# A hybrid layer's recurrences on TensorE: Gated DeltaNet's two directions in one pass, RWKV-7's head halves alternating

## The chip, the cores and the metric

One core of a Trainium2 chip runs the whole program in one launch. The metric is the device time of an execution in microseconds (us). The engines are PE (TensorE: matrix products and transposes), DVE (VectorE), ACT (ScalarE), POOL (GpSimd) and SP (SyncE, whose queue issues most DMAs). PEld is PE's loading of weights, which a trace shows apart. On-chip memory has 128 partitions; PSUM, the memory that products are written to, has eight banks.

## The reference

One layer: a token mixer of four branches on the same modulated input (256 context and 256 latent tokens, 2048 channels), then a gated ConvFFN. Cut to the two branches that the change touches:

```python
def gdn_scan(q, k, v, lg, beta, S):       # both directions stacked; chunks of 64 tokens
    """S_t = a_t S_{t-1}(I - b_t k_t k_t^T) + b_t k_t v_t^T (S: (G,H,dk,dv)), o_t = S_t^T q_t."""
    ...
    def step(S, inp):
        ut, wt, at, qt, kt, glt = inp
        vnew = ut - jnp.einsum('ghld,ghde->ghle', wt, S)
        o = jnp.einsum('ghld,ghde->ghle', qt, S) + jnp.einsum('ghts,ghse->ghte', at, vnew)
        S = S * jnp.exp(glt)[..., None, None] + jnp.einsum('ghld,ghle->ghde', kt, vnew)
        return S, o

def rwkv_scan(r, w, k, v, a, b, S):       # 8 heads of 64
    def step(S, inp):
        rt, wt, kt, vt, at, bt = inp
        sa = jnp.einsum('ghij,ghj->ghi', S, at)
        S = S * wt[:, :, None, :] + sa[..., None] * bt[:, :, None, :] + vt[..., None] * kt[:, :, None, :]
        return S, jnp.einsum('ghij,ghj->ghi', S, rt)
```

DeltaNet has 4 heads of 128 channels; the forward direction takes the chunks in order, the backward one in reverse, first over the context (no outputs wanted), then over the latent tokens from the state the context left. The other branches are a convolution module and a bidirectional mLSTM. Their four outputs are projected, weighted by sigmoid gates, summed (the merge) and projected once more.

## The kernel before

Everything large is a product with streamed weights. A weight block is loaded as `raw` through SP's queue, ACT rounds it to `hi` (line 192), DVE takes the rest `lo` (line 194), and PE multiplies three times: hi by the input's high part (`uh`), hi by its low part (`ul`), lo by `uh`. Results with weights stationary are psB, with activations stationary psA. adaLN's products (psw) are spread between them. The recurrences are in plain fp32; each fp32 product appears in the trace as two records, a transpose as one.

The order on each engine is set by the framework's scheduler, which lists the instructions by simulated times of its own. The recurrences are given to it with priority, and what is left of PE's time is filled with column sets: psB for the branches' columns, psA for the gates, and, beside the mLSTM, the merges.

- RWKV-7 (`rw_unit`, `rw_step`, both directions' chunks in turn): `rw_unit` prepares one chunk of 64 tokens. The 8 heads lie as 4 pairs (h) on two halves of the partitions (q). For each q, four products psG (one PSUM bank for each q, tag "u", which has two banks), a masked copy G on DVE, a copy to AL on ACT; then four transposes psT for each q. 16 units in all. psS, psY and psSA, in `rw_step`, are written with h outside and q inside.
- DeltaNet (`gd_scan`): two segments (context, latent) of four chunks. In each, for i in 0 to 3 and each direction d: pKS = K S (4 heads), gX = V - decay pKS on DVE, pVN = U gX (U: a triangular inverse made before), gVN = beta pVN, for the latent segment pQS = Q S and pO = att gVN, both into the output `go`, then pSn = K^T gVN and the new state gS on DVE. A chunk's rows lie on the half of the partitions given by the chunk's parity; direction d at step i uses one half alone, and the DVE instructions run on 64 partitions. Kd and V are loaded for two chunks (128 tokens) at a time.
- mLSTM (`ml_scan`): four chunks of 128 in two half steps each (one a direction): psr (row terms), masks mA made by ACT and DVE from psr and the scores psq, psn = mA V, then dn and mlh on DVE. Its output goes through `head_out` (squares mhsq, mhms, transposes psho).
- Merge (`merge`): 16 sets of 24 psA products, in order of the branches RWKV, convolution, DeltaNet, mLSTM. The first branch's sets are written to the accumulator mg (line 1327), the others added on POOL (line 1330) after a product with the gate (line 1329).

Tiles live in pools, stacks of on-chip memory: a pool opened later lies above those still open, and takes over the place of one that has been closed; who takes over a place waits for its last reader.

Of the kernel before, what the change touches and what calls it, by code (L numbers as in the profile page):

```python
# [11 lines left out]
F32 = mybir.dt.float32  # L12
# [3 lines left out]
AF = mybir.ActivationFunctionType  # L16
# [4 lines left out]
P = 128  # L21
# [11 lines left out]
# columns of the per-channel parameters: first one, number  # L33
# [8 lines left out]
class Kern:  # L42
# [4 lines left out]
    # ---------------------------------------------------------------- helpers  # L47
# [13 lines left out]
    def aux(self, name="aux", tag="aux"):  # L61
        """PSUM bank; its tag's banks go round in program order."""
        bufs = self.auxn.get(tag)
        assert bufs, tag
        return self.auxp.tile([P, 512], F32, tag=tag, name=name, bufs=bufs)
# [8 lines left out]
    def evp(self, name):  # L74
        """PSUM behind column sets and adaLN, apart from the recurrences'."""
        return self.wap.tile([P, 512], F32, tag="wa", name=name)
# [3 lines left out]

    def tr(self, out, in_, b=0):
        """out = in_.T; in_ starts at partition b."""
        k = in_.shape[0]
        self.nc.tensor.transpose(out, in_, self.ident[b : b + k, b : b + k])
# [9 lines left out]
    def rsqrt(self, pool, x, shape, tag):  # L94
        """x ** -0.5 in place of a small fp32 tile of positive values (Newton from a bit-level guess)."""
# [6 lines left out]
        # y (15 - 10 a + 3 a^2) / 3 of a = x y^2, then y' (3 - 9/64 x y'^2) 3/16  # L102
# [9 lines left out]
    # ---------------------------------------------------------------- constants  # L112
    def constants(self):
# [15 lines left out]
        # LM[:, kind, col] over (row % 64): 0 col>row, 1 col>=row, 2 col<row, 3 col<=row  # L129
# [7 lines left out]
        # block-diagonal 128x128 versions  # L137
# [19 lines left out]
    def first_params(self):  # L157
        """Per-channel parameters, one column per 128 channels; c and c_ctx first."""
        t = self.cp.tile([P, NVEC], F32, name="vec")
        for sl in (slice(0, 32), slice(32, NVEC)):  # L160
            self.nc.sync.dma_start(out=t[:, sl], in_=self.A["vec"][:, sl])
        self.PC = {nm: t[:, o : o + n] for nm, (o, n) in VEC.items()}

    def params(self):
        nc, PC = self.nc, self.PC
        # a = 1 - mu0 - mu1 of the token shift
# [10 lines left out]
    # ---------------------------------------------------------------- weight stream  # L177
# [3 lines left out]
    def load_split(self, parts, width, rings=None):  # L181
        """parts: [(dram [256, w], column offset)] -> hi, lo tiles [128, 2, 512] in fp32r."""
# [18 lines left out]
    def mode_b_steps(self, parts_of, width, blocks, uh, ul, nkt, bank=None):  # L201
        """Weights stationary: out[channel, token]. blocks: (offset, M, token0, N, evacuate).
        One step per pair of K tiles; the evacuations follow the last."""
# [16 lines left out]
    def mode_a(self, parts_of, uh, ul, nkt, toks, evac, apart=0, rings=None):  # L220
        """Activations stationary: out[token, channel] for 512 channels. apart: this many last steps go by token tile."""
# [19 lines left out]
    # ---------------------------------------------------------------- adaLN  # L241
    def wmod_steps(self, cb, dst, raws=None, gain=None):
        """One step per 256 rows of w_mod[:, 512 cb:][:512]; the last one leaves silu(c) @ it + b_mod in dst, feature-major
        [128, 4, 1 or 2]. The partial sums of column half h lie on rows 64 h + 32 k + {0: c, 1: c_ctx}."""
# [18 lines left out]
        if gain is not None:  # L263
            # a gate vector on every partition, times the norm's gain
# [25 lines left out]
    def mod_feed(self):  # L290
        """Steps of the other four adaLN vectors of the latent stream, taken beside the column sets: shift and scale of the
        FFN feature-major, the gates token-major."""
# [6 lines left out]
    def feed(self, upto=0):  # L299
        """As many adaLN steps as the rate says, and all before step `upto`."""  # L300
# [5 lines left out]
    # ---------------------------------------------------------------- phase 0  # L306
    def phase0(self, first, opened):
        """adaLN shift and scale of the mixer, modulated input u (context tokens first); `first`: the steps of
        column sets that run as its K tiles appear; `opened`: called before their last ones."""
# [38 lines left out]
        # what is left of u takes the place of the token tiles  # L348
# [42 lines left out]
    # ---------------------------------------------------------------- inverse of unit triangular 64x64 blocks  # L391
# [7 lines left out]
    def tinv(self, pool, tag, d, n, N, U, pool_rec=False, ptag="aux"):  # L399
        """U[:, j] = (I - N[:, j])^-1 for n matrices per half of the partitions: rows s on partitions (two blocks  # L400
        of 64), columns t on the free axis; N is read only where t follows s (t > s for d = 0, t < s for d = 1).
        U's off-diagonal block on the other side has to be zero already. A generator: what needs no product first."""
# [78 lines left out]
    # ---------------------------------------------------------------- RWKV-7  # L481
    def shift(self, out3, ps3, nm, i, M):
        """Token shift of out3 [M, segments, 256] from PSUM."""
# [6 lines left out]
    def stage(self, tag, shape, name):  # L490
        """Staging tile behind a column set."""
# [3 lines left out]
    def rw_k_steps(self):  # L495
# [3 lines left out]
        def ev_k(i):  # L499
            def f(ps):  # L500
                k, kk = self.kT[:, i], self.kk[:, i]
                self.shift(s3(k), s3(ps), "", 4 + i, P)
                # -l2_normalize(k * rw_kk) per head
# [14 lines left out]
    def rw_ev_v(self, i):  # L518
        """Evacuation of a block of v: feature-major latent half, token-major to DRAM."""
# [57 lines left out]
    def rw_feat(self):  # L577
        """Decayed operands of all chunks, per direction: dAR [.., chunk, head pair, a | r], dBK [.., b | k | b]."""
# [6 lines left out]
        # 0 at the multiples of 64, 1 elsewhere  # L585
# [5 lines left out]
        for h in range(4):  # L591
# [39 lines left out]
            # bonus = sum over the head of r * (kmod of both directions) * rk, times v  # L631
# [7 lines left out]
    def rw_unit(self, d, ch):  # L639
        """Masked products and triangular inverses of one chunk of 64 tokens."""  # L640
# [13 lines left out]
        G = [wp.tile([P, 4, P], F32, tag="G%d" % i, name="G%d" % i) for i in range(2)]  # L654
        for q in range(2):
            ps = self.aux("psG", "u")
            p3 = ps[:, 0 : 4 * W_].rearrange("p (h t) -> p h t", h=4)
            r, o = half[q], half[1 - q]
            for h in range(4):
                self.mm(p3[:, h], bk[r, h, 64 * q : 64 * q + P], AL[q][r, h, 0:W_])  # L660
            nc.vector.tensor_tensor(G[q][:, :, 0:W_], p3, mb, ALU.mult)
            nc.scalar.activation(AL[q][o, :, 0:W_], G[q][o, :, 0:W_], AF.Copy)
        bkT = wp.tile([P, 2, 4, 64], F32, tag="bkT", name="bkT")
        for q in range(2):
            ps = self.aux("psT", "u")
            p3 = n4(ps)
            for h in range(4):
                self.tr(p3[:, h], bk[half[q], h, 64 * q : 64 * q + P], 64 * q)
            nc.scalar.activation(bkT[:, q], p3, AF.Copy)
# [6 lines left out]
    def rw_sv(self, d, ch):  # L676
        """New [S^T ; V] tile of a chunk: V in place."""
# [6 lines left out]
    def rw_step(self, d, ch, unit, SV, nxt):  # L684
        """One chunk: reads SV, writes the states into the next SV (None behind the last chunk)."""
# [82 lines left out]
    # ---------------------------------------------------------------- branch outputs  # L768
    def put_y(self, n, b, yf):
        """Block b (128 channels) of branch n's output, split for the projection; kept where u's context half was."""  # L770
# [4 lines left out]
    def head_norm(self, pool, tag, h, n_tok, nh, w, eps):  # L775
        """rsqrt(mean(h^2) + eps) over the last axis of h [128, n_tok, nh, w] -> [128, n_tok, nh]."""
# [9 lines left out]
    def head_out(self, pool, tag, h, gate, norm, n):  # L786
        """Branch n = rms_norm(h [128, 2, 4, 128]) * norm * gate [128 channels, 4, 256]."""
# [6 lines left out]
        for b in range(4):  # L794
            ps = self.aux("psho")
            for i in range(2):
                self.tr(ps[:, P * i : P * i + P], h[:, i, b])
# [4 lines left out]
    # ---------------------------------------------------------------- convolution module  # L802
# [41 lines left out]
    def conv_module(self):  # L844
# [26 lines left out]
        for i in range(4):  # L871
            nc.vector.tensor_tensor(acc[:, i], acc[:, i], mean, ALU.subtract)
            sq = cp.tile([P, 256], F32, tag="csg", name="csq", bufs=2)
# [12 lines left out]
    # ---------------------------------------------------------------- gate scalars, token-major  # L886
    def token_gates(self, gp):
        """lg [128, 4 tiles, 8], beta, and mLSTM's li, lf, all (direction, head) on the last axis."""
# [10 lines left out]
        g = gp.tile([P, 4, 2, 2, 2, 4], F32, name="gtok")  # tile, (ml, gd), direction, (i/f or a/b), head  # L899
# [11 lines left out]
        # softplus(x) = max(x, 0) + log1p(exp(-|x|)), log1p(y) = 2 atanh(y / (2 + y))  # L911
# [21 lines left out]
    # ---------------------------------------------------------------- gated DeltaNet  # L933
    def gd_columns(self):
# [56 lines left out]
        def ev_q(h):  # L991
            def f(ps):
# [4 lines left out]
                # sums over the channels, tokens on partitions  # L997
# [10 lines left out]
    def gd_scan(self):  # L1008
# [9 lines left out]
        # decays: inclusive sums, sums after a token, chunk totals  # L1018
# [17 lines left out]
        nc.vector.tensor_scalar(fl(nbeta), fl(beta), -1.0, None, ALU.mult)  # L1036
        self.dbg("egc", egc)
        self.dbg("erem", erem)
        self.dbg("egl", egl)
        N = up.tile([P, 2, 2, 4, 64], F32, name="gN")     # direction, tile of the segment, head, t  # L1040
# [9 lines left out]
        for seg in range(2):  # L1050
# [33 lines left out]
            order = [[0, 1, 2, 3], [3, 2, 1, 0]]  # L1084
            KV = [None, None]
            for i in range(4):
                for d in range(2):
                    c = order[d][i]
                    jj, j = c // 2, 2 * seg + c // 2
                    r = slice(64 * (c % 2), 64 * (c % 2) + 64)  # L1090
                    if i % 2 == 0:
# [577 lines left out]
```

## Time and profile before

| | |
|---|---|
| median of 3 runs | 2360.63 us (2359.28 to 2361.23) |
| profiled execution, span | 2358.9 us |
| PE busy | 2250.4 us (95%) |
| DVE, ACT, POOL busy | 1478.0, 987.1, 500.8 us |
| moved by DMA | 471.97 MB, 200 GB/s on average |
| RWKV's scan (psG, psS and the like) | about 324 to 757 us |
| DeltaNet's steps | 928 to 968 and 1110 to 1230 us |
| mLSTM's scan | about 1290 to 1403 us |

The profiled execution's span lies 1.7 us below the runs' median, 0.4 us below the fastest run. A row of the timeline gives the start, the duration, the engine, the line, the operation and how many records it groups; the time from one row's start to the next one's is what the engine was held for. Line 79 is the helper that issues all products, line 84 the one for transposes.

### The profile page before, as it was taken

To read this page: it belongs to the slowest core of one execution; us is meant where nothing else is said; L and a number is where in the kernel's file an instruction comes from. 1 tells how busy PE (TensorE), PEld (TensorE's weight loads), DVE (VectorE), ACT (ScalarE), POOL (GpSimd) and SP (SyncE) were. 2 spreads that over 40 slices of the span, in tenths; PEclk is the share of its full clock that TensorE was granted. 3 is DMA by queue.
4 is the path that set the end of the run, shared out by engine and by line. 5 is a ranking of instruction groups with operands and counts; after the bars stand their busy time and mean duration, and the time that the engine had idled before them with its cause. 6 is when DMAs were issued, how large, how long until landed. Compare 5 with 4: busy or idle time off the path is not lost.

```text
span 2358.9 us, 42865 instructions
## 1 busy us (share of the span) xinstructions
PE 2250.4 (95%) x16820; PEld 1846.2 (78%) x16820; DVE 1478.0 (63%) x3079; ACT 987.1 (42%) x1491; POOL 500.8 (21%) x849
## 2 busy tenths in 40 slices
PE   6979899999999899999999999989999999999998
PEld 3657677877888666767777777779999999998886
DVE  3357866643555976566556478566777677775554
ACT  4225644433444343233225544444444344444443
POOL 0012563533452995000001034010000000000000
PEclk8989899899999999999999999989999999999999
DMA  9934654454666677677668667567767666666563
GB/s 367 347 113 129 180 166 117 133 169 135 184 180 197 184 239 216 208 238 233 189 206 275 185 223 262 184 224 216 225 210 218 208 182 187 180 199 204 193 195 101
DMA packets 273612, 471.97 MB, mean 200 GB/s; under 512 B 41505, under 2 KB 80673, under 8 KB 272417
## 3 DMA queue, kind: packets, MB, share of 16 engines
q1 hardware_dynamic: 273122, 467.14, 63.6%
q8 instruction: 132, 2.16, 0.4%
q10 hardware_dynamic: 288, 2.10, 0.2%
q14 instruction: 70, 0.57, 0.1%
HBM read 440.33 MB, written 28.84 MB: 199 GB/s over the span
## 4 chain that ended last, share of the span: by engine, by line
PE 80%; DVE 8%; DMA 5%; ACT 2%; POOL 2%; issue 2%; SPq 0%; DVEq 0%; ACTq 0%; POOLq 0%
PE psB L79 35%; PE psA L79 20%; PE psD L79 10%; PE psw L79 4%; DVE lo L194 2%; DMA wraw<-in_w_mod 2%; PE psG L79 1%; DMA raw<-in_w_mix 1%; DVE cacc L858 1%; POOL riU L397 1%; PE pVN L79 1%; PE pKS L79 1%; PE pSn L79 1%; ACT hi L192 1%; PE psf L79 1%
## 5 line engine op out<-in xcount | busy, mean ns | idle before, releaser
L194 DVE TENSOR_TENSOR lo<-raw,hi 128x1024 fp32r<-128x1024 f32 (+2 forms) x485 | 603.6, 1246 | 449.7 <-ACT hi L192 440.2
L192 ACT ACTIVATE hi<-raw 128x1024 fp32r<-128x1024 f32 (+2 forms) x488 | 508.4, 1043 | 845.4 <-PE psB L79 383.7
L79 PE MATMUL psB<-u2h,lo 128*128 128x256 f32 x1408 | 396.7, 283 | 0.0
L79 PE MATMUL psB<-u2l,hi 128*128 128x256 f32 x1408 | 396.5, 283 | 0.2 <-DVE u2l L1354 0.2
L79 PE MATMUL psB<-u2h,hi 128*128 128x256 f32 x1408 | 395.5, 285 | 1.1 <-DVE u2h L1353 1.1
L79 PE MATMUL psA<-lo,uh 128*128 128x512 f32 x832 | 336.3, 405 | 12.6 <-DVE lo L194 12.3
L79 PE MATMUL psA<-hi,ul 128*128 128x512 f32 x832 | 329.8, 397 | 0.0
L79 PE MATMUL psA<-hi,uh 128*128 128x512 f32 x832 | 310.0, 404 | 2.2 <-ACT hi L192 2.2
L79 PE MATMUL psB<-uh,hi 128*128 128x256 f32 (+1 forms) x832 | 281.5, 347 | 24.4 <-ACT hi L192 17.8
L79 PE MATMUL psB<-ul,hi 128*128 128x256 f32 (+2 forms) x832 | 278.9, 340 | 0.0
L79 PEld LDWEIGHTS psB<-u2h,hi 128*128 128x128 f32 x1408 | 267.6, 192 | 10.8 <-issue 9.5
L79 PEld LDWEIGHTS psB<-u2l,hi 128*128 128x128 f32 x1408 | 269.9, 192 | 0.5 <-DVE u2l L1354 0.5
L79 PEld LDWEIGHTS psB<-u2h,lo 128*128 128x128 f32 x1408 | 269.8, 192 | 0.1
L79 PE MATMUL psB<-uh,lo 128*128 128x256 f32 (+2 forms) x832 | 263.1, 342 | 6.8 <-DVE lo L194 6.8
L79 PEld LDWEIGHTS psA<-lo,uh 128*128 128x128 f32 x832 | 156.9, 189 | 63.0 <-DVE lo L194 21.7
L79 PEld LDWEIGHTS psB<-uh,hi 128*128 128x128 f32 x832 | 159.9, 193 | 54.8 <-ACT hi L192 20.7
L79 PEld LDWEIGHTS psA<-hi,uh 128*128 128x128 f32 x832 | 153.5, 189 | 51.5 <-issue 15.0
L79 PEld LDWEIGHTS psA<-hi,ul 128*128 128x128 f32 x832 | 157.0, 189 | 33.6 <-issue 1.0
L79 PEld LDWEIGHTS psB<-uh,lo 128*128 128x128 f32 (+1 forms) x832 | 153.8, 192 | 32.3 <-DVE lo L194 9.6
L79 PEld LDWEIGHTS psB<-ul,hi 128*128 128x128 f32 (+1 forms) x832 | 160.6, 193 | 22.0 <-issue 6.1
L1524 DVE TENSOR_TENSOR lo<-raw,hi 128x1024 fp32r<-128x1024 f32 x88 | 107.6, 1225 | 78.3 <-ACT hi L1523 78.2
L1444 DVE SCALAR_TENSOR_TENSOR facc<-fpad,ffdw,facc 128x256 f32<-128x256 f32 x352 | 152.9, 488 | 0.2
(569 smaller groups left out, 3129.1 us busy)
## 6 DMA issues: line engine op xcount, KB each, us to landing
raw<-in_w_in SPq DMA_DIRECT2D x208, 512.0 KB, 4.5
raw<-in_ffn_up SPq DMA_DIRECT2D x176, 512.0 KB, 3.9
wraw<-in_w_mod SPq DMA_DIRECT2D x160, 512.0 KB, 5.3
raw<-in_ffn_down SPq DMA_DIRECT2D x88, 512.0 KB, 4.6
raw<-in_w_br SPq DMA_DIRECT2D x32, 512.0 KB, 4.8
raw<-in_w_out SPq DMA_DIRECT2D x32, 512.0 KB, 4.7
raw<-in_w_mod SPq DMA_DIRECT2D x32, 512.0 KB, 4.0
raw<-in_w_in SPq DMA_DIRECT2D x48, 256.0 KB, 3.7
```

The costliest lines, as they stand in the source:

```text
L79: self.nc.tensor.matmul(out, lhsT, rhs, start=start, stop=stop)
L192: nc.scalar.activation(hi[s], raw[s], AF.Copy)
L194: (nc.gpsimd if self.pool_lo >= 0 else nc.vector).tensor_tensor(lo[s], raw[s], hi[s].bitcast(F32), ALU.subtract)
L397: eng.tensor_tensor(U16[:, :, t], U16[:, :, t], m[:, :, t], ALU.add)
L858: nc.vector.scalar_tensor_tensor(a, cpad[:, i, t : t + 256], w(i, t), a, ALU.mult, ALU.add)
L1444: nc.vector.scalar_tensor_tensor(s3(acc), pad[:, dy : dy + 4, dx : dx + 64], tap(t, b), s3(acc), ALU.mult, ALU.add)
L1524: nc.vector.tensor_tensor(f(lo), f(raw), f(hi).bitcast(F32), ALU.subtract)
```

## The change

1. A helper `mms` issues a list of products with their order on PE locked against the scheduler. Other instructions may still be put between them.
2. `rw_unit` takes both banks of psG at once and lets the two halves q alternate within each head pair; psT likewise.
3. `gd_scan` takes both directions in one pass: at step i, chunk i of the forward and chunk 3 - i of the backward direction, which always lie on opposite halves. Products of the same kind alternate between the directions; the DVE instructions run once on 128 partitions instead of twice on 64, gS excepted. Kd and V are loaded per step in halves. Four new tiles `gm...` hold the decays and beta in the order in which the joint steps want them, filled by 16 small POOL copies. `go` is kept with its halves crossed, and `head_out` sorts that out by products with a permuted identity.
4. The tile csq of the convolution module shares the tag of another.

```diff
+    def mms(self, products):
+        with self.tc.manual_schedule(engines={mybir.EngineType.PE}):
+            for out, lhsT, rhs in products:
+                self.mm(out, lhsT, rhs)
...
     def rw_unit(self, d, ch):
-        for q in range(2):
-            ps = self.aux("psG", "u")
-            p3 = ps[:, 0 : 4 * W_].rearrange("p (h t) -> p h t", h=4)
-            r, o = half[q], half[1 - q]
-            for h in range(4):
-                self.mm(p3[:, h], bk[r, h, 64 * q : 64 * q + P], AL[q][r, h, 0:W_])
+        p3 = [self.aux("psG", "u")[:, 0 : 4 * W_].rearrange("p (h t) -> p h t", h=4) for q in range(2)]
+        pairs = [(h, q) for h in range(4) for q in range(2)]
+        self.mms((p3[q][:, h], bk[half[q], h, 64 * q : 64 * q + P], AL[q][half[q], h, 0:W_]) for h, q in pairs)
...
     def gd_scan(self):
+        m4 = {}
+        for nm, src in (("negc", negc), ("egc", egc), ("erem", erem), ("beta", beta)):
+            t = m4[nm] = gp.tile([P, 2, 4, 4], F32, name="gm" + nm)
+            f = src.rearrange("p (s j) d h -> p s (j d) h", s=2)
+            for r, pairs in ((slice(0, 64), ((0, 1, 0, 1), (1, 4, 3, 0))), (slice(64, P), ((0, 1, 3, 4), (1, 4, 0, 3)))):
+                for a, b, x, y in pairs:
+                    o = f[r, :, x:y] if x < y else f[r, :, x:y:-1]
+                    nc.gpsimd.tensor_scalar(t[r, :, a:b], o, 1.0, None, ALU.mult)
...
             for i in range(4):
+                ch = [i, 3 - i]
+                R = [slice(64 * (c % 2), 64 * (c % 2) + 64) for c in ch]
+                both = [(h, d) for h in range(4) for d in range(2)]
...
+                pk = v4(self.aux("pKS"))
+                self.mms((pk[R[d], h], kT[:, h, tk[d]], S[d][:, h]) for h, d in both)
+                X = wp.tile([P, 4, P], F32, tag="X", name="gX", bufs=1)
+                for h in range(4):
+                    nc.vector.scalar_tensor_tensor(X[:, h], pk[:, h], m4["negc"][:, seg, i, h : h + 1], V[:, h], ALU.mult, ALU.add)
+                pv = v4(self.aux("pVN"))
+                self.mms((pv[R[d], h], U[R[d], d, ch[d] // 2, h], X[R[d], h]) for h, d in both)
+                VN = wp.tile([P, 4, P], F32, tag="VN", name="gVN", bufs=1)
+                nc.vector.tensor_tensor(VN, pv, b4(m4["beta"][:, seg, i]), ALU.mult)
...
+                if seg == 0 or i < 3:
+                    pS = [v4(self.aux("pSn")) for d in range(2)]
+                    self.mms((pS[d][:, h], Kd[R[d], h], VN[R[d], h]) for h, d in both)
+                    for d in range(2):
+                        e = egl[:, ch[d] % 2, 2 * seg + ch[d] // 2, d]
+                        for h in range(4):
+                            nc.vector.scalar_tensor_tensor(S[d][:, h], S[d][:, h], e[:, h : h + 1], pS[d][:, h], ALU.mult, ALU.add)
...
-            sq = cp.tile([P, 256], F32, tag="csg", name="csq", bufs=2)
+            sq = cp.tile([P, 256], F32, tag="ctap", name="csq", bufs=2)
```

What the two programs' orders show at three places follows. A row is one instruction, or several alike.

PE at a DeltaNet step of the context segment, before: one direction's products (4) at a time, the two gS tiles (one for each direction) in turn.

```order
L79 MATMUL pVN<-gX,gU 64x128 x4
L79 MATMUL psA<-lo,uh 128x512
L79 MATMUL psA<-hi,ul 128x512
L79 MATMUL psw<-wraw,cst 32x256 x4
...
L79 MATMUL pSn<-gVN,gKd 128x128 x4
L79 MATMUL pKS<-gS_9264,gkT 64x128 x4
L79 MATMUL psA<-hi,uh 128x512 x2
```

After:

```order
L79 MATMUL pVN<-gX,gU 64x128 x8
L79 MATMUL psf<-sel_74,wrows 128x4 x2
...
L79 MATMUL pSn<-gVN,gKd 128x128 x8
L79 MATMUL psw<-wraw,cst 32x256 x4
...
L79 MATMUL pKS<-gS_9379,gkT 64x128
L79 MATMUL pKS<-gS_9380,gkT 64x128
```

The products stand in blocks of eight, the two directions' states alternating, with column products between the blocks.

PE at psG of one RWKV unit, before (AL_3572 and AL_3573 are the two halves q):

```order
L79 MATMUL psG<-AL_3572,bk 128x64 x4
L79 MATMUL psgq<-ones,gsq 128x1 x2
L79 MATMUL psB<-uh,lo 128x512
...
L79 MATMUL psG<-AL_3573,bk 128x64 x4
L84 MATMUL psT<-ident,bk 128x64 x4
```

After, at a later unit:

```order
L79 MATMUL psG<-AL_4052,bk 128x128
...
L79 MATMUL psG<-AL_4053,bk 128x128
L79 MATMUL psG<-AL_4052,bk 128x128
L79 MATMUL psG<-AL_4053,bk 128x128
```

The first product stands alone, with filler behind it, and the other seven follow in one run; so it is in 14 of the 16 units, in two all eight stand together.

PE at the mLSTM's last half step, before (one psr, filler, one psn, filler):

```order
L79 MATMUL psr<-mlr_11191,mlsel 128x256 x2
L79 LDWEIGHTS idb
L79 MATMUL psr<-mlmask,idb 128x256
L79 MATMUL psA<-hi,uh 128x512 x2
...
L79 MATMUL psA<-hi,ul 128x512
L79 MATMUL psn<-mv,mA 128x129 x7
L79 MATMUL psA<-hi,uh 128x512 x2
```

After, the last two half steps:

```order
L79 MATMUL psr<-mlr_11292,mlsel 128x256 x2
L79 LDWEIGHTS idb
L79 MATMUL psr<-mlmask,idb 128x256
L79 MATMUL psn<-mv,mA 128x129 x7
L79 MATMUL psr<-mlr_11324,mlsel 128x256 x2
L79 LDWEIGHTS idb
L79 MATMUL psr<-mlmask,idb 128x256
L79 MATMUL psn<-mv,mA 128x129 x7
L79 MATMUL psA<-hi,uh 128x512
```

The merge's psA products that stood there have moved behind the last psn. DVE at the same place, before:

```order
L1244 TENSOR_TENSOR mA<-mA,psq_11395 128x512
L1245 TENSOR_TENSOR mA<-mA,psq_11396 128x256
L1248 TENSOR_TENSOR mA<-mA,psq_11396 128x128
L194 TENSOR_TENSOR lo<-raw,hi 128x1024
L1329 TENSOR_TENSOR sig<-sig,psA 128x512 x2
L194 TENSOR_TENSOR lo<-raw,hi 128x1024
L1257 TENSOR_TENSOR dn<-dn,mlem 128x2
L1258 RECIPROCAL dn<-dn 128x2
L1263 SCALAR_TENSOR_TENSOR mlh<-psn,dn,mlh 128x128 x2
```

After:

```order
L1261 TENSOR_TENSOR mA<-mA,psq_11528 128x512
L1262 TENSOR_TENSOR mA<-mA,psq_11529 128x256
L1265 TENSOR_TENSOR mA<-mA,psq_11529 128x128
L1274 TENSOR_TENSOR dn<-dn,mlem 128x2
L1275 RECIPROCAL dn<-dn 128x2
L1280 SCALAR_TENSOR_TENSOR mlh<-psn,dn,mlh 128x128 x2
L1344 TENSOR_TENSOR mg<-sig,psA 128x512 x4
```

No `lo` and no merge instruction stands between the last mA and mlh any more; the first write of mg (line 1344 of the changed kernel) follows the last mlh, where the kernel before has four sets written earlier. In the changed program mA's place in the on-chip memory overlaps mg's; before, the two lay apart.

More of the change, by code (lines that the diff above doesn't have):

```diff
@@ L654, in rw_unit @@
         G = [wp.tile([P, 4, P], F32, tag="G%d" % i, name="G%d" % i) for i in range(2)]
+        p3 = [self.aux("psG", "u")[:, 0 : 4 * W_].rearrange("p (h t) -> p h t", h=4) for q in range(2)]
+        pairs = [(h, q) for h in range(4) for q in range(2)]
+        self.mms((p3[q][:, h], bk[half[q], h, 64 * q : 64 * q + P], AL[q][half[q], h, 0:W_]) for h, q in pairs)
         for q in range(2):
-            ps = self.aux("psG", "u")
-            p3 = ps[:, 0 : 4 * W_].rearrange("p (h t) -> p h t", h=4)
-            r, o = half[q], half[1 - q]
-            for h in range(4):
-                self.mm(p3[:, h], bk[r, h, 64 * q : 64 * q + P], AL[q][r, h, 0:W_])
-            nc.vector.tensor_tensor(G[q][:, :, 0:W_], p3, mb, ALU.mult)
+            o = half[1 - q]
+            nc.vector.tensor_tensor(G[q][:, :, 0:W_], p3[q], mb, ALU.mult)
             nc.scalar.activation(AL[q][o, :, 0:W_], G[q][o, :, 0:W_], AF.Copy)
         bkT = wp.tile([P, 2, 4, 64], F32, tag="bkT", name="bkT")
+        p3 = [n4(self.aux("psT", "u")) for q in range(2)]
+        with self.tc.manual_schedule(engines={mybir.EngineType.PE}):
+            for h, q in pairs:
+                self.tr(p3[q][:, h], bk[half[q], h, 64 * q : 64 * q + P], 64 * q)
         for q in range(2):
[L665 to L669, printed above, removed]
+            nc.scalar.activation(bkT[:, q], p3[q], AF.Copy)
         U = self.rwU[d][self.rwi[d] % 3]
@@ L784, in head_norm, with head_out @@
         return self.rsqrt(pool, ms, [P, n_tok, nh], tag + "r")
-    def head_out(self, pool, tag, h, gate, norm, n):
+    def head_out(self, pool, tag, h, gate, norm, n, crossed=False):
         nc = self.nc
@@ L795, in head_out @@
             ps = self.aux("psho")
+            p4 = ps[:, 0:256].rearrange("p (x c) -> p x c", c=64)
             for i in range(2):
-                self.tr(ps[:, P * i : P * i + P], h[:, i, b])
+                if crossed:
+                    self.mm(p4[:, 2:0:-1] if i else p4[:, 0:4:3], h[:, i, b], self.ident.rearrange("p (x c) -> p x c", c=64))
+                else:
+                    self.tr(ps[:, P * i : P * i + P], h[:, i, b])
             yf = pool.tile([P, 256], F32, tag=tag + "yf", name=tag + "yf", bufs=2)
@@ L1083, in gd_scan @@
                 list(self.tinv(tp, "gi", d, 8, m(N), m(U)))
-            order = [[0, 1, 2, 3], [3, 2, 1, 0]]
-            KV = [None, None]
             for i in range(4):
-                for d in range(2):
[L1088 to L1091, printed above, removed]
-                        Kd = wp.tile([P, 4, P], F32, tag="Kd", name="gKd")
-                        V = wp.tile([P, 4, P], F32, tag="V", name="gV")
-                        t = slice(P * j, P * j + P)
-                        nc.sync.dma_start(out=Kd, in_=self.dK[t])
-                        nc.sync.dma_start(out=V, in_=self.dV[t])
-                        nc.gpsimd.tensor_tensor(Kd, Kd, b4(erem[:, j, d]), ALU.mult)
-                        KV[d] = (Kd, V)
-                    Kd, V = KV[d]
-                    v4 = lambda ps: ps.rearrange("p (h e) -> p h e", h=4)
-                    tk = slice(64 * c, 64 * c + 64)
-                    pk = v4(self.aux("pKS"))
-                    for h in range(4):
-                        self.mm(pk[r, h], kT[:, h, tk], S[d][:, h])
-                    X = wp.tile([P, 4, P], F32, tag="X", name="gX", bufs=1)
-                    for h in range(4):
-                        nc.vector.scalar_tensor_tensor(X[r, h], pk[r, h], negc[r, j, d, h : h + 1], V[r, h], ALU.mult, ALU.add)
-                    pv = v4(self.aux("pVN"))
-                    for h in range(4):
-                        self.mm(pv[r, h], U[r, d, jj, h], X[r, h])
-                    VN = wp.tile([P, 4, P], F32, tag="VN", name="gVN", bufs=1)
-                    nc.vector.tensor_tensor(VN[r], pv[r], b4(beta[r, j, d], 64), ALU.mult)
-                    if seg:
-                        pq = v4(self.aux("pQS"))
-                        for h in range(4):
-                            self.mm(pq[r, h], qT[:, h, tk], S[d][:, h])
-                        if i < 2:
-                            nc.vector.tensor_tensor(go[r, jj], pq[r], b4(egc[r, j, d], 64), ALU.mult)
-                        else:
-                            for h in range(4):
-                                nc.vector.scalar_tensor_tensor(go[r, jj, h], pq[r, h], egc[r, j, d, h : h + 1], go[r, jj, h], ALU.mult, ALU.add)
-                        po = v4(self.aux("pO"))
-                        for h in range(4):
-                            self.mm(po[r, h], att[r, d, jj, h], VN[r, h])
-                        nc.vector.tensor_tensor(go[r, jj], go[r, jj], po[r], ALU.add)
-                    if seg == 0 or i < 3:
-                        pS = v4(self.aux("pSn"))
-                        for h in range(4):
-                            self.mm(pS[:, h], Kd[r, h], VN[r, h])
-                        for h in range(4):
-                            nc.vector.scalar_tensor_tensor(S[d][:, h], S[d][:, h], egl[:, c % 2, j, d, h : h + 1], pS[:, h], ALU.mult, ALU.add)
@@ new lines, in gd_scan @@
+                ch = [i, 3 - i]
+                R = [slice(64 * (c % 2), 64 * (c % 2) + 64) for c in ch]
+                tk = [slice(64 * c, 64 * c + 64) for c in ch]
+                both = [(h, d) for h in range(4) for d in range(2)]
+                Kd = wp.tile([P, 4, P], F32, tag="Kd", name="gKd")
+                V = wp.tile([P, 4, P], F32, tag="V", name="gV")
+                for d in range(2):
+                    t = slice(256 * seg + 64 * ch[d], 256 * seg + 64 * ch[d] + 64)
+                    nc.sync.dma_start(out=Kd[R[d]], in_=self.dK[t])
+                    nc.sync.dma_start(out=V[R[d]], in_=self.dV[t])
@@ new lines, in gd_scan @@
+                nc.gpsimd.tensor_tensor(Kd, Kd, b4(m4["erem"][:, seg, i]), ALU.mult)
+                v4 = lambda ps: ps.rearrange("p (h e) -> p h e", h=4)
+                pk = v4(self.aux("pKS"))
[3 more added lines that the diff above has]
+                    nc.vector.scalar_tensor_tensor(X[:, h], pk[:, h], m4["negc"][:, seg, i, h : h + 1], V[:, h], ALU.mult, ALU.add)
@@ new lines, in gd_scan @@
+                pv = v4(self.aux("pVN"))
+                self.mms((pv[R[d], h], U[R[d], d, ch[d] // 2, h], X[R[d], h]) for h, d in both)
+                VN = wp.tile([P, 4, P], F32, tag="VN", name="gVN", bufs=1)
+                nc.vector.tensor_tensor(VN, pv, b4(m4["beta"][:, seg, i]), ALU.mult)
+                if seg:
+                    g = go[:, (0, 1, 1, 0)[i]]
+                    pq = v4(self.aux("pQS"))
+                    self.mms((pq[R[d], h], qT[:, h, tk[d]], S[d][:, h]) for h, d in both)
+                    if i < 2:
+                        nc.vector.tensor_tensor(g, pq, b4(m4["egc"][:, seg, i]), ALU.mult)
+                    else:
+                        for h in range(4):
+                            nc.vector.scalar_tensor_tensor(g[:, h], pq[:, h], m4["egc"][:, seg, i, h : h + 1], g[:, h], ALU.mult, ALU.add)
+                    po = v4(self.aux("pO"))
+                    self.mms((po[R[d], h], att[R[d], d, ch[d] // 2, h], VN[R[d], h]) for h, d in both)
+                    nc.vector.tensor_tensor(g, g, po, ALU.add)
@@ L1135, in gd_scan @@
         nc.vector.tensor_scalar(rq, rq, float(P ** -0.5), None, ALU.mult)
-        for i in range(2):
-            nc.vector.tensor_tensor(go[:, i], go[:, i], b4(rq[:, i]), ALU.mult)
+        for c in range(2):
+            r = slice(64 * c, 64 * c + 64)
+            for i in range(2):
+                nc.vector.tensor_tensor(go[r, i], go[r, i], b4(rq[r, (i + c) % 2], 64), ALU.mult)
         self.dbg("go", go)
@@ L1142, in gd_out @@
         es = ExitStack()
-        self.head_out(self.pool("ghp", stack=es), "gh", go, self.gz, "gd_norm_g", 2)
+        self.head_out(self.pool("ghp", stack=es), "gh", go, self.gz, "gd_norm_g", 2, crossed=True)
         es.close()
```

## The prediction

> **What bounds the kernel now.** I read the page's busy times and its chain of waits first, then PE's busy share by stretch, then single rows of PE in the three recurrences.
>
> ```profile
> PE 2250.4 (95%) x16820; PEld 1846.2 (78%) x16820; DVE 1478.0 (63%) x3079; ACT 987.1 (42%) x1491; POOL 500.8 (21%) x849
> PE 80%; DVE 8%; DMA 5%; ACT 2%; POOL 2%; issue 2%; SPq 0%; DVEq 0%; ACTq 0%; POOLq 0%
> ```
>
> The second line is the chain that ended last: PE is the bound, and a microsecond of PE time is worth about one of the span wherever PE is full. The windows (start:end, length, PE busy, count, granted clock, DMA share, GB/s) show that it is full where the change acts: RWKV's scan, DeltaNet's two segments, and the mLSTM scan behind them.
>
> ```profile
> 320.00:760.00 440.00, 431.61 (x4778) 0.98 0.52 154
> 928.00:968.00 40.00, 40.00 (x256) 1.00 0.70 210
> 1110.00:1230.00 120.00, 119.67 (x729) 1.00 0.64 196
> 1290.00:1403.00 113.00, 113.00 (x570) 1.00 0.68 217
> ```
>
> So the recurrences' latency is covered by column products (psA, psB) put between their steps, and what counts is how long PE is held by their small products. One DeltaNet step shows that (start, duration, then count; each fp32 product has two records):
>
> ```profile
> 934.82 1.08 PE L79 MATMUL pVN<-gX,gU 64*64 64x128 f32 x8
> 935.83 0.50 PE L79 MATMUL psA<-lo,uh 128*128 128x512 f32 x1
> ...
> 940.04 1.16 PE L79 MATMUL pSn<-gVN,gKd 64*128 64x128 f32 x8
> 941.13 1.09 PE L79 MATMUL pKS<-gS,gkT 128*64 128x128 f32 x8
> 942.15 0.73 PE L79 MATMUL psA<-hi,uh 128*128 128x512 f32 x2
> ```
>
> From start to next start a run of eight holds PE 1.01, 1.09 and 1.02 us. Runs whose neighbours lie on opposite halves of the partitions stand against it:
>
> ```profile
> 661.97 1.16 PE L79 MATMUL psG<-AL,bk 64*128 64x128 f32 x8
> 663.06 0.56 PE L79 MATMUL psY<-SV,AL 128*64 128x64 f32 x10
> ...
> 324.39 1.60 PE L79 MATMUL psG<-AL,bk 64*128 64x64 f32 x16
> 325.92 0.50 PE L79 MATMUL psB<-uh,lo 128*128 128x512 f32 x1
> ...
> 601.27 0.69 PE L79 MATMUL psS<-SV,bkT 128*64 128x64 f32 x16
> 601.89 0.33 PE L79 MATMUL pa<-riTD,rioff 32*32 32x32 f32 x16
> ...
> 483.66 0.68 PE L79 MATMUL psSA<-RH,rwU 64*64 64x64 f32 x14
> 484.26 0.64 PE L79 MATMUL psw<-wraw,cst 128*32 128x256 f32 x8
> ```
>
> psG on one half of the rows costs 1.09 us for eight records. psS and psSA, written h outside and q inside, alternate halves: sixteen in 0.62 us, fourteen in 0.60, 39 to 43 ns each. At 324.39 two runs of psG met and about half of the sixteen alternate: 1.53 us instead of 2 x 1.09 = 2.18. If eight cost the serial 1.09 and the others the rest, an alternating psG record costs (1.53 - 1.09) / 8 = 55 ns. It loads 128 columns of weights, as pSn does.
>
> By the Trainium skill's "TensorEngine Tiling (Array Packing)", Gotcha 1: PSUM Pressure, different row tiles cannot access the same PSUM bank at once. pVN and pO, where the change puts two row halves in one bank, would then stay serial. psSA is such a case here (both halves in one bank, on opposite partitions) and takes 43 ns a record, so the trace speaks against that for this pattern.
>
> **The change part by part.** The groups by form (count | busy, mean ns) give the numbers of records:
>
> ```profile
> L79 PE MATMUL pVN<-gX,gU 64*64 64x128 f32 x128 | 18.6, 278 | 0.0
> L79 PE MATMUL psG<-AL,bk 64*128 64x128 f32 x128 | 18.5, 285 | 0.0
> L79 PE MATMUL psG<-AL,bk 64*128 64x64 f32 x128 | 18.1, 296 | 0.0
> L79 PE MATMUL pKS<-gS,gkT 128*64 128x128 f32 x128 | 17.8, 280 | 0.0
> L79 PE MATMUL pSn<-gVN,gKd 64*128 64x128 f32 x112 | 16.2, 285 | 0.0
> L84 PE MATMUL psT<-ident,bk 64*128 64x64 f32 x128 | 14.5, 238 | 0.0
> L79 PE MATMUL pQS<-gS,gqT 128*64 128x128 f32 x64 | 9.8, 283 | 0.0
> L79 PE MATMUL pO<-gVN,gatt 64*64 64x128 f32 x64 | 8.7, 275 | 0.0
> ```
>
> *DeltaNet's products.* 128 + 128 + 64 + 64 + 112 = 496 records are 62 runs of eight, at a mean of 1.04 us 64.5 us. After: 31 runs of sixteen. A run of eight is 8 x 0.11 = 0.9 us of steps and 0.2 us of entry and end, which I keep; at 55 ns a run of sixteen takes 0.2 + 0.88 = 1.08, all of them 33.5. Gain 31 us. Bounds: 31 x 1.53 = 47.4, a gain of 17; at psSA's 43 ns 31 x 0.89 = 27.6, a gain of 37. I take 55 ns, since these stream 128 columns as against psSA's 64.
>
> *RWKV.* psG's 256 records are 32 runs of eight, 34.9 us. The new order sends most units as one product (two records, 0.2 + 0.22 us), filler, then seven in one run (14 records: 0.2 + 0.77), 1.4 us against 2.18: 14 such units gain 11 us, and two contiguous ones (1.08) 2 us. psT is smaller (14.5 us busy in all); I put 0.1 us on each of its 16 pairs, 2 us. Together 15; bounds 5 (as at 324.39) and 19 (at 43 ns).
>
> *DeltaNet's chain.* Both directions now wait for each other: a step is pKS, gX, pVN, gVN, pSn, gS, and no second chain lies beside it. Its DVE parts:
>
> ```profile
> L1107 DVE SCALAR_TENSOR_TENSOR gX<-pKS,negc,gV 64x128 f32<-64x128 f32 x64 | 18.3, 348 | 0.5 <-PE pKS L79 0.2
> L1131 DVE SCALAR_TENSOR_TENSOR gS<-gS,egl,pSn 128x128 f32<-128x128 f32 x56 | 15.7, 341 | 10.0 <-PE pSn L79 9.9
> L194 DVE TENSOR_TENSOR lo<-raw,hi 128x1024 fp32r<-128x1024 f32 (+2 forms) x485 | 603.6, 1246 | 449.7 <-ACT hi L192 440.2
> ```
>
> gX on 128 partitions costs 4 x 0.35 = 1.4 us for both, gS 8 x 0.34 = 2.7. A `lo` of 1.25 may stand ahead. The new order puts some 5 us of filler between pKS and pVN, 3 before pSn, 4 before the next pKS. Only the last is short: 2.7 + 1.25 + a landing of 0.1 to 0.3 against 4. At 0 to 0.6 us in seven steps I take 2 us (bounds 0 and 4). DVE loses 32 gX (11 us) and 8 gVN (5.5 us) and gains two small scalings; it is not the bound in these windows, so this is worth nothing by itself.
>
> *Loads, copies, tags.* Eight more DMA issues on SP's queue (Kd and V by halves, the same bytes, one step ahead), 16 small POOL copies before the first step, and csq's tag: nothing, since the filler above stands between steps and DMA's share is 0.64 to 0.70. What the scheduler shuffled in the first 120 us I bound by 5 us either way.
>
> *The memory's layout.* The four gm tiles take 4 x 128 = 512 bytes a partition in the pool that stands below nearly all others, and everything above slides up. The mLSTM's ring of mA tiles no longer fits at the top and lands, in the changed program, on the bytes of mg, the merge's accumulator. So no write of mg can precede the last mA. Before, seven sets of merge products lie between the mLSTM's half steps; after, the four banks fill up, and the order shows nothing between psr and psn in the last three half steps. What those take without cover is in these rows (PE, ACT and DVE of one half step, then the scan's end):
>
> ```profile
> 1383.21 1.13 PE L79 MATMUL psr<-mlr,mlsel 4*128 4x256 f32 x4
> 1384.27 0.28 PE L79 MATMUL psr<-mlmask,idb 128*128 128x256 bf16 x1
> 1386.40 0.28 DVE L1248 TENSOR_TENSOR mA<-mA,psq 128x128 f32<-128x128 f32 x1
> ...
> 1401.52 1.72 PE L79 MATMUL psn<-mv,mA 128*128 128x129 f32 x14
> ...
> 1405.78 0.61 DVE L1263 SCALAR_TENSOR_TENSOR mlh<-psn,dn,mlh 128x128 f32<-128x128 f32 x2
> 1407.29 0.69 DVE L782 TENSOR_REDUCE mhms<-mhsq 128x4 f32<-128x512 f32 x1 [0.90 <-POOL mhsq L781]
> 1420.06 1.29 DVE L793 TENSOR_TENSOR mlh<-mlh,mhry 128x512 f32<-128x512 f32 x2
> ```
>
> psr ends at 1384.55 and the last mA at 1386.68: 2.1 us in which an uncovered PE idles, with landings and the dn and mlh of the half before 2.5 to 3. Three times that is 8.5. Behind the last psn the next psA needs a bank, so it waits for dn, mlh and the first mg: 2.2. From there to psho lie two squares, two reductions, a dozen DVE instructions and 1.29, some 10 us from the last psn, under which the order has 24 psA (5.5 us): 2.2 more. Sum 13 (bounds 7 and 25; before, 1405.78 to 1421.3 lay under 72 psA, and if none of it were covered the stretch alone is 15).
>
> Idle PE also lost its clock:
>
> ```profile
> 441.61 0.24 PE L79 MATMUL pd<-riD,riM 32*32 32x32 f32 x2 [2.20 <-DVE riM L90]
> 443.00:455.00 12.00, 12.00 (x64) 0.50 0.37 111
> 765.00:771.00 6.00, 3.77 (x20) 0.72 0.89 332
> ```
>
> After 2.2 us of idling at 439 the granted clock was 0.50 for twelve microseconds. The mLSTM's tail has four or five such gaps with some 16 us of PE work among them; at half clock on a quarter of it, 4 us (bounds 0 and 16).
>
> By the Trainium skill's "TensorE: Matmul & The Clock Gate", Part 1, the clock halves after an idle window of about 3.4 us that runs freely. By that rule the tail's gaps of 2 to 3 us would mostly cost no clock, and the sum below would be 2331; the drop here came after 2.2 us, and the sum goes by that row.
>
> **The sum.** 2358.9 - 31 - 15 + 2 + 13 + 4 = 2332.9 us for the profiled span. The runs' median is 2360.63, 1.7 above that span: 2335 us, 1.1% less.
>
> **Rivals.**
> (a) Full gain: the mLSTM's tail is covered (mA's place costs nothing, say because POOL and DVE catch up). 2360.6 - 46 + 2 = 2317. Against it stands the order with its three bare half steps.
> (b) Row halves don't overlap within one bank: pVN and pO (24 of 62 runs, 25 us) keep their time. 11.7 us less gain: 2347. psSA speaks against it; that psSA has 64 columns leaves room. (By the rule of the Trainium skill's "TensorEngine Tiling (Array Packing)" quoted above it would come out so.)
> (c) No change: alternation brings only what the half-met run at 324.39 shows (17 + 5 = 22), against 19 of cost: 2358. That run was only half alternating, which makes it a lower bound.
> (d) Slower: each of the 31 joint DeltaNet blocks stands at PE's head waiting for DVE, because one `lo` of 1.25 us more than the scheduler thought is ahead of gX, gVN or gS, and the other direction no longer fills that time. 31 x 1.25 = 39 us on top of 2335: 2374. It decides from 26 / 31 = 0.8 us a block on. For it: DVE takes its queue in order, and the two segments keep it about half busy. Against it: 3 to 5 us of filler stand before each block.
>
> **How the numbers follow.** My forecast has 0.52, (a) 0.14, (b) 0.14, (c) 0.08, (d) 0.12. No change means within 0.2%, 4.7 us, about what this kernel's runs can tell (their spread is 2 us): (c) half of it and a little of (b)'s and my own upper end, 0.09. Slower: (d), 0.12. Faster: the rest, 0.79. My forecast's own range, with tail and clock at their bounds, is 2322 to 2352. The range of 8 in 10 takes in (a) with the upper bound of the products (2313) and (c), and ends at 2361; below and above it are left 0.05 and 0.13.
>
> **What would show it.** pKS, pVN and pSn as runs of sixteen of 0.9 to 1.2 us; psG's run of fourteen near 1.0; PE idle between psr and psn in the last three mLSTM half steps, with mg written only behind the last mA; waits of PE for gS under 1 us a step. I am wrong if runs of sixteen take 2 us, if PE waits for gX or gVN at each step, or if the mLSTM's tail costs above 30 us.

## The result, and the profile after

The changed kernel takes 2328.26 us (median of 4 runs, 2325.89 to 2336.68) against 2359.95 before (4 runs): a ratio of 0.9869, 95% interval 0.9849 to 0.9888, so 1.3% faster; 2335 had been forecast. Measured once more in a later set it took 2326.53 against 2362.75, 0.9846 (0.9831 to 0.9861). The profiled spans are 2327.1 and 2358.9 us, 31.8 apart.

The page's busy times of the changed kernel, and its windows (start:end, length, PE busy, count, granted clock, DMA share, GB/s) at RWKV's scan, DeltaNet's two segments, and the mLSTM's first and last part:

```profile
PE 2215.9 (95%) x16828; PEld 1812.0 (78%) x16828; DVE 1449.6 (62%) x3027; ACT 989.5 (43%) x1493; POOL 507.6 (22%) x865
...
320.00:760.00 440.00, 434.13 (x4865) 0.99 0.57 168
960.00:1000.00 40.00, 39.72 (x302) 1.00 0.78 234
1110.00:1190.00 80.00, 78.78 (x667) 1.00 0.74 216
1252.00:1310.00 58.00, 58.00 (x294) 1.00 0.64 198
1310.00:1350.00 40.00, 30.39 (x131) 0.79 0.26 88
```

PE is as full as before, with 34.5 us less to do, except in the last line: 10 of 40 us idle, at a clock of 0.79. A DeltaNet step in the timeline:

```profile
968.12 1.09 PE L79 MATMUL pVN<-gX,gU 64*64 64x128 f32 x16
969.14 0.61 PE L79 MATMUL psf<-sel,wrows 128*128 128x4 f32 x4
...
972.81 1.16 PE L79 MATMUL pSn<-gVN,gKd 64*128 64x128 f32 x16
973.90 0.64 PE L79 MATMUL psw<-wraw,cst 128*32 128x256 f32 x8
...
977.90 1.09 PE L79 MATMUL pKS<-gS,gkT 128*64 128x128 f32 x16
978.93 0.51 PE L79 MATMUL psA<-lo,uh 128*128 128x512 f32 x1
```

Sixteen records hold PE 1.02, 1.09 and 1.03 us, as long as eight did before, and no wait stands at any of them. The single records behind these rows show how: in pVN's and pSn's runs before, one record starts every 109 to 112 ns; now two start in that time, 6 or 7 ns apart, by the order one of each direction. The groups by form have the same counts as before and less busy time (line 90 is now the helper for transposes):

```profile
L79 PE MATMUL psG<-AL,bk 64*128 64x128 f32 x128 | 13.1, 291 | 0.0
L79 PE MATMUL psG<-AL,bk 64*128 64x64 f32 x128 | 11.4, 280 | 0.0
L90 PE MATMUL psT<-ident,bk 64*128 64x64 f32 x128 | 11.2, 240 | 0.0
L79 PE MATMUL pKS<-gS,gkT 128*64 128x128 f32 x128 | 10.0, 281 | 0.0
L79 PE MATMUL pVN<-gX,gU 64*64 64x128 f32 x128 | 9.4, 278 | 0.0
L79 PE MATMUL pSn<-gVN,gKd 64*128 64x128 f32 x112 | 8.1, 285 | 0.0
```

Counted from each run's first start to the next operation's start, DeltaNet's five products went from 66.3 to 35.2 us, psG from 32.0 to 22.4 and psT from 11.4 to 9.1.

The mLSTM's end, where the order had been shown bare of filler (PE's rows, with the idle time before them in brackets):

```profile
1318.17 0.28 PE L79 MATMUL psr<-mlmask,idb 128*128 128x256 bf16 x1
1320.28 1.20 PE L79 MATMUL psn<-mv,mA 128*128 128x129 f32 x4 [1.82 <-DVE mA L1261]
...
1325.83 1.10 PE L79 MATMUL psr<-mlr,mlsel 4*128 4x256 f32 x4 [0.60 <-DVE mlh L1280]
1326.86 0.28 PE L79 MATMUL psr<-mlmask,idb 128*128 128x256 bf16 x1
1328.88 2.31 PE L79 MATMUL psn<-mv,mA 128*128 128x129 f32 x14 [1.74 <-ACT mA L1259]
1332.65 2.04 PE L79 MATMUL psr<-mlr,mlsel 4*128 4x256 f32 x4 [1.47 <-DVE mlh L1278]
1334.62 0.39 PE L79 MATMUL psr<-mlmask,idb 128*128 128x256 bf16 x1
1336.81 3.35 PE L79 MATMUL psn<-mv,mA 128*128 128x129 f32 x14 [1.79 <-ACT mA L1259]
1342.25 0.50 PE L79 MATMUL psA<-hi,uh 128*128 128x512 f32 x1 [2.09 <-DVE mg L1344]
```

The gaps add up to 9.5 us, and the last is the wait for mg. In between the products slow down: the last run of psn's fourteen records took 1.72 us before; here the last two take 2.31 and 3.35.

### The profile page after: what moved, and what is told of

It reads as the page before. It is cut to its first block, busy times and chain, and to the rows that moved or that the text cites. A ratio compares the mean times of both kernels' runs of the same rounds, so it can differ in the third digit from the quotient of the medians.

```text
span 2327.1 us, 42867 instructions
## 1 busy us (share of the span) xinstructions
PE 2215.9 (95%) x16828; PEld 1812.0 (78%) x16828; DVE 1449.6 (62%) x3027; ACT 989.5 (43%) x1493; POOL 507.6 (22%) x865
## 4 chain that ended last, share of the span: by engine, by line
PE 78%; DVE 8%; DMA 7%; POOL 4%; ACT 2%; issue 2%; SPq 0%; DVEq 0%; ACTq 0%; POOLq 0%
PE psB L79 37%; PE psA L79 18%; PE psD L79 10%; PE psw L79 4%; DMA wraw<-in_w_mod 3%; DVE lo L200 2%; POOL ctap L874 1%; DMA raw<-in_w_mix 1%; PE psG L79 1%; POOL cacc L875 1%; ACT hi L198 1%; PE psn L79 1%; DMA raw<-in_w_in 1%; PE psf L79 1%; DVE cacc L869 1%
## 5 line engine op out<-in xcount | busy, mean ns | idle before, releaser
L79 PEld LDWEIGHTS psA<-hi,uh 128*128 128x128 f32 x832 | 154.7, 190 | 53.2 <-issue 12.2
L79 PEld LDWEIGHTS psB<-uh,lo 128*128 128x128 f32 (+1 forms) x832 | 152.8, 189 | 32.0 <-DVE lo L200 10.5
```

The lines of the kernel that those rows point to most:

```text
L79: self.nc.tensor.matmul(out, lhsT, rhs, start=start, stop=stop)
```

## The experiments

The kernel before took 2361.05 us beside the first four experiments and 2362.75 us beside the last three; each ratio is to those runs.

**mA and mg apart.**

```diff
-            t = m4[nm] = gp.tile([P, 2, 4, 4], F32, name="gm" + nm)
+            t = m4[nm] = up.tile([P, 2, 4, 4], F32, name="gm" + nm)
```

> The changed kernel with one difference: the four gm tiles are taken from the pool of the segment's inverses (closed with the scan) instead of the long-lived pool below everything, so that mA and mg lie apart again as in the kernel before. Theory (mA on mg's bytes bares the mLSTM's tail): the psA products are back between the last half steps, the 9.5 us of gaps and the half clock there go, and the time falls by 12 to 16 us from 2328, to about 2314. Rival (the tail is bare because the joint DeltaNet steps used up the filler): the tail stays bare and the time stays at 2325 to 2331.

Measured: 2309.42 us, 0.9782 of before (0.9762 to 0.9803). The same place in its timeline, and its windows:

```profile
1346.08 1.13 PE L79 MATMUL psr<-mlr,mlsel 4*128 4x256 f32 x4
1347.14 0.28 PE L79 MATMUL psr<-mlmask,idb 128*128 128x256 bf16 x1
1352.79 1.72 PE L79 MATMUL psn<-mv,mA 128*128 128x129 f32 x14
...
1330.00:1340.00 10.00, 10.00 (x49) 1.00 0.49 159
1340.00:1350.00 10.00, 10.00 (x47) 1.00 0.68 213
```

No wait, full clock, and 5.4 us of psA between psr and psn. The products' times are those of the changed kernel (psG 22.4 us, pKS 9.3, pSn 7.6). The gain over the changed kernel, 17 to 19 us by its two measurements, is more than the 12 to 16 expected. The change could thus have given 52 us, and lost those 17 to 19 by where four small tiles lay. This version is the fastest of all that were run.

**The layout alone.** The kernel before, plus

```diff
+        for nm in ("negc", "egc", "erem", "beta"):
+            t = gp.tile([P, 2, 4, 4], F32, name="gm" + nm)
+            nc.gpsimd.memset(t, 0.0)
...
-            sq = cp.tile([P, 256], F32, tag="csg", name="csq", bufs=2)
+            sq = cp.tile([P, 256], F32, tag="ctap", name="csq", bufs=2)
```

> The kernel before with four dead tiles of 128 bytes a partition in the long-lived pool (and csq sharing its tag as in the change, which makes room): nothing of the products changes. Theory: the layout alone bares the mLSTM's last three half steps, 12 to 16 us more than before, about 2374. Rival (layout has nothing to do with it): 2358 to 2362.

Measured: 2377.07 us, 1.0061 of before (1.0046 to 1.0076): 512 unused bytes a partition cost 16 us. The rows are those of the changed kernel:

```profile
1378.95 3.33 PE L79 MATMUL psn<-mv,mA 128*128 128x129 f32 x14 [1.74 <-ACT mA L1245]
1383.75 1.10 PE L79 MATMUL psr<-mlr,mlsel 4*128 4x256 f32 x4 [1.47 <-DVE mlh L1264]
1386.86 3.35 PE L79 MATMUL psn<-mv,mA 128*128 128x129 f32 x14 [1.79 <-ACT mA L1245]
1392.30 0.80 PE L79 MATMUL psA<-hi,uh 128*128 128x512 f32 x1 [2.09 <-DVE mg L1330]
```

The joint steps are not in this kernel, and csq's shared tag, which is, stands in the first experiment too, where the tail is covered. The two experiments together show the cause: the layout, not the joint steps.

**RWKV's part alone.** The kernel before with `mms` and the new `rw_unit`; its DeltaNet scan is the old one.

> The kernel before with RWKV's part of the change alone (psG and psT alternating, locked). Theory: psG and psT give 12 us as in the changed kernel, less some 3 us since the order leaves the mLSTM's last half step without psA: 2350 to 2353. Rival (RWKV's part gives nothing, its products only moved): 2358 to 2362.

Measured: 2357.89 us (median of 10 runs), 0.9984 (0.9972 to 0.9996): 3 us, less than the 8 to 11 expected. psG and psT did fall as expected (22.4 and 9.1 us), but the tail of the mLSTM was barer than I had read from the order:

```profile
1413.72 1.80 PE L79 MATMUL psn<-mv,mA 128*128 128x129 f32 x14 [1.47 <-DVE mA L1250]
1416.99 1.10 PE L79 MATMUL psr<-mlr,mlsel 4*128 4x256 f32 x4 [1.46 <-DVE mlh L1267]
1420.04 3.35 PE L79 MATMUL psn<-mv,mA 128*128 128x129 f32 x14 [1.74 <-ACT mA L1248]
1430.92 1.54 PE L90 MATMUL psho<-ident,mlh 128*128 128x128 f32 x6 [7.54 <-DVE mlh L799]
```

12.2 us of gaps, 7.5 of them before psho, though mA and mg lie apart here. RWKV's scan ends 25 us later in the execution than in the kernel before (its last psSA at 776.8 against 751.3), since more column products were put into it (1567 records of psB against 1311). I take it that what was used there was missing at the mLSTM's end: its last half step has no psA where the kernel before has 48, and the half step before it has 2 between psr and psn where that kernel has 14. The first experiment's scan holds the same 1567, and its mLSTM is covered; there the joint DeltaNet steps are shorter, and fewer psA are spent between RWKV's scan and the mLSTM's (1368 against 1548 here). That more filler would mend it wasn't tried on this kernel.

**No alternation.** As the first experiment, with

```diff
-        pairs = [(h, q) for h in range(4) for q in range(2)]
+        pairs = [(h, q) for q in range(2) for h in range(4)]
...
-                both = [(h, d) for h in range(4) for d in range(2)]
+                both = [(h, d) for d in range(2) for h in range(4)]
```

> As the first of this set (mA and mg apart), joint DeltaNet steps and locked products as in the change, but the products of one direction (of one half q in RWKV) stand one behind the other instead of alternating. Theory (alternation is the gain): a run of sixteen costs 0.2 + 16 x 0.11 = 1.96 us instead of 1.03, 31 runs 29 us, RWKV's 12 us are lost too: 41 us above the first of this set, about 2355. Rival (one pass, with half the runs and half the DVE instructions, is the gain): within 12 us of the first, 2315 to 2327.

Measured: 2346.05 us, 0.9928 (0.9911 to 0.9945), 36.6 us above the first experiment. The order inside the blocks is most of the gain. One step:

```profile
938.64 1.58 PE L79 MATMUL pVN<-gX,gU 64*64 64x128 f32 x16
944.16 1.71 PE L79 MATMUL pSn<-gVN,gKd 64*128 64x128 f32 x16
```

1.6 to 1.7 us, not the 1.96 expected: where one direction's products end and the other's begin, neighbours lie on opposite halves and overlap, as in psG's run at 324.39 before. In the single records of pVN's run a second row of starts, 109 ns apart like the first, begins 5 ns after the run's fifth record; I read it as the second direction's, so that four records of each run side by side. DeltaNet's products take 51.0 us here against 35.2; one pass without alternation already saves 15 of the 31 us.

**DeltaNet's part alone.** As the first experiment, with `rw_unit` as before.

> The kernel with mA and mg apart, but with RWKV's unit as before: DeltaNet's part of the change alone. The order keeps 24 psA between the mLSTM's last half steps. Theory (RWKV's alternation is worth its 12 us of PE wherever the tail keeps its filler, and gave only 3 us alone because the mLSTM's end ran out of it): 12 us above the 2309 of both parts, 2319 to 2324. Rival (RWKV's part is worth 3 us or so anywhere): 2309 to 2314.

Measured: 2329.33 us, 0.9859 (0.9845 to 0.9874), 20 us above the first experiment where 10 to 15 were expected. So RWKV's part is worth even more than its 12 us of psG and psT where the tail keeps its filler: psSA, psY, psR and the inverse's pa, whose runs are cut less often, take 5.5 us less too (12.5, 11.4, 12.1 and 9.1 us with it; 13.6, 12.5, 13.2 and 11.3 without; idle time left out), and PE idles 6.5 us less over the whole program (104.4 against 110.9). That is 24 us; other products, psA above all, take some of it back.

**No lock.** As the first experiment, with `mms` and the transposes outside the locked schedule.

```diff
-        with self.tc.manual_schedule(engines={mybir.EngineType.PE}):
-            for out, lhsT, rhs in products:
-                self.mm(out, lhsT, rhs)
+        for out, lhsT, rhs in products:
+            self.mm(out, lhsT, rhs)
```

> The kernel with mA and mg apart and both parts of the change written as they are, but with no lock on PE's order. The order shows DeltaNet's blocks alternating all the same, and psG and psT in fours, one half q behind the other, as before the change. Theory (the lock matters for RWKV alone): as the kernel with DeltaNet's part alone, 2319 to 2324. Rival (the lock costs PE waits at its blocks, which go without it): below 2309.

Measured: 2334.89 us, 0.9879 (0.9862 to 0.9895), 5.6 us above DeltaNet's part alone, though the two intervals overlap, and well above the 2319 to 2324 expected. The groups by form:

```profile
L79 PE MATMUL psG<-AL,bk 64*128 64x128 f32 x128 | 18.5, 285 | 0.0
L79 PE MATMUL psG<-AL,bk 64*128 64x64 f32 x128 | 16.5, 289 | 0.0
...
L79 PE MATMUL pVN<-gX,gU 64*64 64x128 f32 x128 | 8.7, 276 | 0.0
```

DeltaNet's blocks alternate without a lock (its five products take 34.6 us, as with DeltaNet's part alone), while psG and psT fall apart into fours. So the lock is what makes RWKV's part work, and DeltaNet's gain doesn't depend on it. PE idles 4.5 us more here than with DeltaNet's part alone (115.4 against 110.9); why wasn't followed up.

**The changed kernel again.**

> The changed kernel itself once more, on the same chip and against the same runs as the other two. By the first measurement 2328 (2326 to 2337); both theories expect that it stays between 2323 and 2335, 12 to 20 us above the kernel with mA and mg apart.

Measured: 2326.53 us, as told above, 17 us above the first experiment.

## Why the prediction was right, step by step

*DeltaNet's products, 31 us.* 66.3 to 35.2, 31.1 us. The 55 ns taken from psG's half-met run were right: two records start every 109 to 112 ns. With entry and end that is 64 ns a record, 1.02 to 1.09 us a run against 1.08.

*RWKV, 15 us.* 9.6 for psG and 2.3 for psT, 12. psG's time after the change came as worked out (22.4 us against some 22); what was too high is the time before, 32 runs at 1.09 us or 34.9, where the trace has 32.0. Two pairs of runs had met there, as at 324.39, and in eight of the 16 units the last psG overlap with the first psT. What was missed are the 5.5 us of RWKV's other products, which stand in longer runs now. With those the term was 17.4.

*DeltaNet's chain, 2 us.* Nothing: PE's list of waits names no gX, gVN or gS. The slower rival (d), a wait of 0.8 us or more at each block, did not occur at all.

*The tail's idle time, 13 us.* 9.5 us: 7.4 in the half steps for 8.5, 2.1 at the first mg for 2.2, and nothing ahead of psho, where 2.2 had been put. *The clock, 4 us*: idle time left out, psn takes 15.5 us instead of 12.2, psr 10.5 instead of 8.8 and psq 7.8 instead of 6.3, 6.5 us more, and some eight psA at half rate another 1.6. A little of this (under 1 us of psr) is the end of a product that filler had covered, the rest is clock, about twice the forecast. Together 17.6 against 17: one term was too high and the other too low, and that they cancel is luck. The two experiments on the layout give 16 to 19.

*The sum.* As recorded it is added up wrongly: its terms give 2331.9 us for the span, not 2332.9, and 2334 for the runs. Its own range doesn't follow from its terms either: tail and clock at their bounds give 2325 to 2359 around 2335. The measured terms, -31.1 - 12 - 5.5 + 9.5 + 6.5 + 1.6 = -31.0, stand against -31.8 of the spans. So close a match is partly chance, for things that no term has cancel out: outside the tail PE idles 6.8 us less than before (all its idle time is 108.5 us before, 111.2 after, of which 9.5 are new), while psw takes 3.1, psA at full rate 2.3 and psho 0.8 us more.

*The rivals.* (a), a covered tail, did not occur, but the first experiment made it: 2309 against the 2317 worked out for it. (b), no overlap in one bank, is out: pVN and pO, both directions in one bank, take 1.02 us a run, pSn in two banks 1.09. That is also against the rule as the Trainium skill's "TensorEngine Tiling (Array Packing)", Gotcha 1: PSUM Pressure, has it. Both row halves writing the same partitions of one bank wasn't tried. (c) is out by the fourth experiment: with runs that only half alternate the kernel takes 37 us more.

Of the 7 us that 2335 stands above 2328, RWKV's term (17.4 for 15) and the chain's 2 us make up 4 and the wrong addition 1; the rest lies in what the sum had no terms for.

## What to carry to other kernels

Small products that use half of the array's rows or columns cost about half when neighbours lie on opposite halves (66.3 to 35.2 us here), so write the loop over the halves innermost, and lock that order where a scheduler might undo it. Where latency is covered by filler, a saving on the bound engine can be lost again if no filler is left for the last chain, as with RWKV's part alone (3 of 12 us): count it there before and after. And look where a new tile moves the others: a few hundred bytes can put two pools on the same place and with that an order between stages that the code doesn't show.

## What the runs showed of the hardware that was not expected

The granted clock fell after gaps shorter than the 2.2 us that the prediction goes by: at the mLSTM's end no gap is longer than 2.1 us, PE is busy 74% and 67% of two stretches, and yet the second runs at half clock throughout (windows of the changed kernel):

```profile
1320.00:1330.00 10.00, 7.38 (x37) 6.08 (x38) 2.91 (x10) 1.90 (x7) 0.00 (x0) 0.84 0.17 54
1330.00:1340.00 10.00, 6.74 (x26) 5.23 (x24) 2.24 (x7) 1.79 (x6) 0.00 (x0) 0.50 0.00 0
```

(Here the columns are the busy times of PE, PEld, DVE, ACT and POOL, each with its count, ahead of the clock.) The Trainium skill's "TensorE: Matmul & The Clock Gate", Part 1, speaks of an idle window of about 3.4 us; several short gaps with little work between did the same here.
